# Deferring the operand forms of four plainly computed column pairs, and regrouping the second half of an MLP

## The chip, the core and the metric

The kernel runs on one core of a Trainium2 chip, as one launch. The metric is device time in microseconds. Engines are named as in the profile: PE is the matrix engine (PEld its weight loads), DVE the vector engine, ACT the scalar engine, POOL the general one, SP the engine on whose queue this kernel issues its DMAs.

## The reference

One step of a two-layer streaming encoder on 1024 prompt tokens and 32 sample tokens (1056 in all, width 1024, float32): layer 0 is a matrix-memory mixer with an MLP, layer 1 a banded attention with an MLP. The change lies in the MLP of layer 1 alone:

```python
x = layer_norm(ALPHA * x + (1 + g1) * y, p['ln_g'][l, 0], p['ln_b'][l, 0])
u = x * (1 + sc2) + sh2
f = jnp.square(jax.nn.relu(u @ p['w_up'][l])) @ p['w_down'][l]      # 1024 -> 4096 -> 1024
x = layer_norm(ALPHA * x + (1 + g2) * f, p['ln_g'][l, 1], p['ln_b'][l, 1])
```

## The kernel before, in words

**Arithmetic.** Every float32 operand is split into a high and a low part (`split`, L87: an ACT copy that rounds, then a DVE subtraction), and a product is three matmuls: high by high, high by low, low by high (`proj`, L110 to L120).

**The MLP of layer 1** (`mlp7`, from L1117) does most of its products with a seven-product scheme for 2 x 2 blocks in place of eight products. The 1056 tokens are four quarters of QN = 264; two quarters make a token pair `tp` (1: the later half, 0: the earlier one). The 4096 hidden columns are 16 column pairs `pb` of 256. A unit (pb, tp) in `Seven` (L1280) has seven products of 12 matmuls each (4 blocks of the contraction by 3). Its weights are seven combinations of the four blocks of a weight tile, made by `forms` (L1240): two loads on SP into the `raw` ring (3 buffers), four sums on DVE, seven splits, into the `wc` ring (6 buffers). Its moving operands are B11, B21, B22 and the combinations T1 to T4 of the activations u, which `tforms` (L1197) makes on DVE and ACT; the last of its steps writes T4 over the block B12 of u.

**Order of "up".** When the norm ahead of the MLP has finished the later half of the tokens, the column pairs 10 to 15 (`L.first`) are computed for that half "plainly", with eight products per block (`up_tile`, L1176; loops at L1313 and L1327); meanwhile the norm of the earlier half is still at work. The steps of `tforms` are spread between these blocks. Then the units follow in the order of `L.seq` (L1866): for the pairs 0 to 9 both token pairs, for 10 to 15 only the earlier half, the "lone" units. Neighbouring units are interleaved on PE by the sort at L1407. `prep` and `advance` (L1389, L1394) issue the weight loads two column pairs ahead and the forms one ahead. Only PE's order is written out by hand; on the other engines a scheduler of the framework lays the operations out, and each engine then works through its own queue in order.

**From "up" to "down".** When a unit or a plain pair is complete, `h_forms` (L1155) squares it on ACT, makes the three sums of the second half's operands on DVE, and splits all seven of them: four into the tile HL, three into HM (one buffer each), which SP stores to DRAM (`hd`). Pairs 14 and 15 (`pb >= NW`) only need a plain split into HL, stored to `hpl`.

**"Down"** takes the pairs 0 to 13 in groups (`GRP`, L1092: first pair and count): 3, 4, 3 and 4 pairs. For each group four units `m` (L1360) compute 256 output columns each, again with seven products, for both token pairs. The 14 operands of a group (7 for each token pair) are loaded into rooms, slots of freed buffers (`Rooms`, L1098; `fill`, L1353): 4 slots of the tile `ext` and 16 of the half of u that is finished are there before "up" ends, the rest after it. The results are added by DVE to the residual ACC (`L.add`, L986), which `L.reload` (L1419 and L1882) brings back from DRAM in four loads right after "up". At the end the pairs 14 and 15 are done plainly (from L1450), with the final norm behind them.

Of the kernel before, what the change touches and what calls it, by code (L numbers as in the profile page):

```python
# [8 lines left out]
F32 = mybir.dt.float32  # L9
# [6 lines left out]
P = 128  # L16
D = 1024
KC = D // P
# [57 lines left out]
def trunk_kernel(ctx: ExitStack, tc: tile.TileContext, a, o):  # L76
# [1012 lines left out]
    QN = T // 4  # L1089
    NPB, KG = 16, 4  # L1090
    NW = 14
    GRP = [(0, 3), (3, 4), (7, 3), (10, 4)]  # L1092
    B11, B22, B21, T1, T2, T4, T3, B12 = range(8)

    PRODS = [(0, B11, 0, 0, 0), (1, B21, 1, 0, 0), (2, T2, 0, 0, 1), (3, T1, 2, 1, 1), (4, T3, 0, 1, 1),
# [28 lines left out]
    def mlp7(L):  # L1124
# [9 lines left out]
        hpl = dr.tile([4, P, 2, T], F32, name=f"hpl{l}")  # L1134
        e_cm = tc.tile_pool(name=f"e{l}", bufs=1, reuse_waits="tile")
        ep = e_cm.__enter__()
        hh_cm = tc.tile_pool(name=f"hh{l}", bufs=1, reuse_waits="tile")
        hhp = hh_cm.__enter__()
        wups, hts = L.wups, {}
# [12 lines left out]
        def h_tile(pb, tp):  # L1152
            return hhp.tile([P, 6, QN], F32, tag="H", name=f"H{l}_{pb}_{tp}", bufs=3)

        def h_forms(pb, tp, H):  # L1155
# [9 lines left out]
            g = [i for i, (p0, kg) in enumerate(GRP) if p0 <= pb][-1]  # L1165
            dst = hd[g][tp][:, :, pb - GRP[g][0]].rearrange("f p l t -> p f (l t)")
            nc.vector.tensor_sub(H[:, 4:6], H[:, 0:3:2], bass.AP(H.tensor, H[:, 1].offset, [H.ap[0], [-QN, 2], [1, QN]]))
# [3 lines left out]
            nc.vector.tensor_sub(H[:, 3], H[:, 3], H[:, 1])  # L1171
            hm = hhp.tile([P, 3, 2, QN], F32R, tag="HM", name=f"HM{l}_{pb}_{tp}", bufs=1)
            split(hm[:, :, 0], hm[:, :, 1], H[:, 1:6:2])
            nc.sync.dma_start(dst[:, 4:7], hm.bitcast(F32).rearrange("p f l t -> p f (l t)"))

        def up_tile(pb, f, q):  # L1176

            tp = q // 2
            ps = up_mm(pb, f, q)
            if (pb, tp) not in hts:  # L1180
                hts[pb, tp] = [h_tile(pb, tp), 0]
            H = hts[pb, tp][0]
            nc.scalar.activation(H[:, ((1, 0), (3, 2))[f][q % 2]], ps, AF.Relu)
            hts[pb, tp][1] += 1
            if hts[pb, tp][1] == 4:
                h_forms(pb, tp, hts.pop((pb, tp))[0])
            flow.tick(QN / 96)

        def up_unit(pb, tp):
# [120 lines left out]

        tp0, tp1 = L.pairs

        TF = {}  # L1313
        for i in range(2):
            L.ready(i)
# [11 lines left out]
        for j, pb in enumerate(rest):  # L1327
            for f in range(2):
                for q in L.quarters[:2]:
                    up_tile(pb, f, q)  # L1330
                if (j, f) == (0, 1):
                    L.ready(2)
                    tiles = L.scratch()
                    TF.update({(tp, i): tiles[2 * n + i] for n, tp in enumerate(L.pairs) for i in range(2)})
                    exts[tp1] = ring.tile([P, 2, KG, QN], F32R, tag="wc", name=f"exu_{l}", bufs=6)
                    tfs = [tf, tforms(tp1, exts[tp1])]
                for n in ((), (0,), (0, 1), (0, 1), (1, 1), (1, 0, 1))[2 * j + f]:
                    next(tfs[n], None)
            del wups[pb]
            if j + 2 < len(rest):  # L1340
                up_w(rest[j + 2])
        def dn_forms(i):
            g, m, _ = units[i]
            p0, kg = GRP[g]
            return forms(lambda s_: w_dn[p0 * 256:(p0 + kg) * 256, m * 256:(m + 1) * 256].rearrange(
                "(k s p) c -> s p k c", s=2, p=P)[s_], kg, f"d{l}_{i}")

        fx, nfx = {}, {}
        order_f = [f for _, f, _, _, _ in PRODS]
        units = [(g, m, [(tp0,), (tp1,)] if g + m == 0 else [(tp0, tp1)]) for g in range(len(GRP)) for m in range(4)]  # L1350
        want = [(tp, f) for tp in L.pairs for f in order_f]

        def fill(g, into):  # L1353
# [27 lines left out]
                        step(i)  # L1381


        seq = L.seq
        jobs = [(n, tp) for n, (pb, tps) in enumerate(seq) for tp in tps]
        makers = [lambda pb=pb: up_forms(pb) for pb, _ in seq] + [lambda i=i: dn_forms(i) for i in range(len(units))]
        preps, got = {}, {}

        def prep(n):  # L1389
            if n < len(makers):  # L1390
                preps[n] = makers[n]()
                next(preps[n])

        def advance(n, i):  # L1394

            if n + 1 in preps and i in (0, 1, 3, 5):
                got[n + 1] = next(preps[n + 1])
            if i == 3:
                prep(n + 2)
        prep(0)  # L1400
        for _ in range(4):
            got[0] = next(preps[0])
        prep(1)
        lone = max(j for j, (_, tp) in enumerate(jobs) if tp == tp0) + 1
        sevens = {}
        with tc.manual_schedule(engines={mybir.EngineType.PE}):
            for _, j, i in sorted((7 * j + 2 * i, j, i) for j in range(len(jobs)) for i in range(7)):  # L1407
                n, tp = jobs[j]
# [451 lines left out]
    class L1:  # L1860
# [91 lines left out]
```

## Time and profile before

| | us |
|---|---|
| median of 3 timed runs (lowest to highest) | 2493.23 (2492.56 to 2494.87) |
| the profiled execution's own time | 2486.63 |
| its span, first to last instruction | 2484.8 |

The mean granted clock of PE in it was 0.984. Busy times by stage, of the profiled execution:

| stage, us from the start | length | PE | DVE | ACT | DMA share | GB/s |
|---|---|---|---|---|---|---|
| plain pairs, 1750.00 to 1787.56 | 37.56 | 37.56 | 37.46 | 32.01 | 0.61 | 214 |
| products of "up", 1827.80 to 2076.00 | 248.20 | 248.20 | 200.99 | 165.90 | 0.70 | 241 |
| its last units, 2076.00 to 2104.00 | 28.00 | 19.90 | 20.44 | 16.67 | 0.77 | 272 |
| start of "down", 2104.00 to 2143.30 | 39.30 | 21.28 | 18.69 | 8.15 | 1.03 | 390 |
| the rest of "down", 2143.30 to 2412.00 | 268.70 | 267.27 | 191.50 | 56.24 | 0.58 | 210 |
| pairs 14, 15 and the final norm, 2412.00 to 2484.80 | 72.80 | 58.69 | 52.80 | 15.09 | 0.32 | 118 |

How to read it: an engine whose busy time equals the length never waited. Matmuls are pipelined, so the duration of one in the trace is longer than the distance to the next; the distances between starts tell the rate. The DMA share is the mean busy share of the core's 16 DMA engines. In rows of the trace, a bracket at the end gives the idle time ahead of the row and what ended it.

### The profile page before, as it was taken

To read this page: it belongs to the slowest core of one execution; us is meant where nothing else is said; L and a number is where in the kernel's file an instruction comes from. 1 tells how busy PE (TensorE), PEld (TensorE's weight loads), DVE (VectorE), ACT (ScalarE), POOL (GpSimd) and SP (SyncE) were. 2 spreads that over 40 slices of the span, in tenths; PEclk is the share of its full clock that TensorE was granted. 3 is DMA by queue.
4 is the path that set the end of the run, shared out by engine and by line. 5 is a ranking of instruction groups with operands and counts; after the bars stand their busy time and mean duration, and the time that the engine had idled before them with its cause. 6 is when DMAs were issued, how large, how long until landed. Compare 5 with 4: busy or idle time off the path is not lost.

```text
span 2484.8 us, 42567 instructions
## 1 busy us (share of the span) xinstructions
PE 2386.1 (96%) x16532; PEld 2293.4 (92%) x16532; DVE 1888.6 (76%) x4228; ACT 1081.7 (44%) x2232; POOL 167.3 (7%) x315
## 2 busy tenths in 40 slices
PE   7999999999999999999999999999979998799997
PEld 4999999999999999999999877799979998799997
DVE  4899999778678778676597667738988888676758
ACT  4644456382211211211366567745756666121212
POOL 0211100000000000000001144400000000000003
PEclk9999999999999999999999999999989999899999
DMA  8433223313224224224123310052546678767632
GB/s 290 128 109 98 82 91 120 116 35 119 77 94 136 78 93 137 77 89 137 51 94 93 90 25 1 18 147 71 199 162 228 234 244 321 279 238 274 254 127 72
DMA packets 246766, 330.95 MB, mean 133 GB/s; under 512 B 12440, under 2 KB 197164, under 8 KB 245028
## 3 DMA queue, kind: packets, MB, share of 16 engines
q1 hardware_dynamic: 246564, 328.23, 39.8%
q8 instruction: 130, 2.13, 0.4%
q14 instruction: 72, 0.59, 0.1%
HBM read 251.31 MB, written 79.24 MB: 133 GB/s over the span
## 4 chain that ended last, share of the span: by engine, by line
PE 77%; DVE 10%; DMA 4%; ACT 2%; issue 1%; POOL 0%; SPq 0%; DVEq 0%; ACTq 0%; POOLq 0%
PE up L1297 10%; PE dn L1375 10%; PE up L118 5%; PE up L120 5%; PE up L119 5%; PE dn L119 5%; PE dn L118 5%; PE dn L120 5%; PE pv L1719 3%; PE s L1662 2%; PE pt L1697 2%; DMA fx<-hd 2%; PE op_a L118 1%; PE op_a L119 1%; PE op_a L120 1%
## 5 line engine op out<-in xcount | busy, mean ns | idle before, releaser
L1375 PE MATMUL dn<-fx,wf_d 128*128 128x264 f32 x2016 | 256.1, 286 | 19.4 <-DMA fx<-hd 16.4
L1375 PEld LDWEIGHTS dn<-fx,wf_d 128*128 128x128 f32 x2016 | 250.5, 190 | 22.0 <-DMA fx<-hd 15.0
L119 PE MATMUL dn<-h,w_dn 128*128 128x384 f32 (+1 forms) x768 | 249.5, 325 | 0.0
L118 PE MATMUL up<-U,w_up 128*128 128x384 f32 (+1 forms) x768 | 249.2, 325 | 0.0
L119 PE MATMUL up<-U,w_up 128*128 128x384 f32 (+1 forms) x768 | 247.9, 323 | 0.0
L118 PE MATMUL dn<-h,w_dn 128*128 128x384 f32 (+1 forms) x768 | 247.8, 323 | 0.0
L120 PE MATMUL up<-U,w_up 128*128 128x384 f32 (+1 forms) x768 | 247.6, 322 | 0.0
L120 PE MATMUL dn<-h,w_dn 128*128 128x384 f32 (+1 forms) x768 | 247.3, 322 | 0.0
L986 DVE SCALAR_TENSOR_TENSOR ACC<-dn,ada,ACC 128x264 f32<-128x264 f32 (+4 forms) x328 | 131.7, 426 | 94.9 <-PE dn L1375 81.8
L238 DVE SCALAR_TENSOR_TENSOR aacc<-rada,cs,aacc 128x256 f32<-128x256 f32 x448 | 190.2, 477 | 0.0
L1297 PE MATMUL up<-u,wf_u 128*128 128x264 f32 x1248 | 169.5, 289 | 20.5 <-ACT wf_u L89 16.5
L1297 PEld LDWEIGHTS up<-u,wf_u 128*128 128x128 f32 x1248 | 160.3, 192 | 22.1 <-ACT wf_u L89 17.2
L986 DVE SCALAR_TENSOR_TENSOR acc<-dn,ada,acc 128x384 f32<-128x384 f32 (+2 forms) x256 | 119.4, 486 | 48.3 <-PE dn L120 47.2
L1025 ACT ACTIVATE r<-up 128x384 f32<-128x384 f32 (+1 forms) x96 | 44.2, 462 | 246.1 <-PE up L120 237.6
L119 PEld LDWEIGHTS dn<-h,w_dn 128*128 128x128 f32 x768 | 144.5, 188 | 0.2 <-DVE h L1028 0.2
L120 PEld LDWEIGHTS dn<-h,w_dn 128*128 128x128 f32 x768 | 144.5, 188 | 0.0
L120 PEld LDWEIGHTS up<-U,w_up 128*128 128x128 f32 x768 | 144.3, 188 | 0.0
L118 PEld LDWEIGHTS up<-U,w_up 128*128 128x128 f32 x768 | 144.2, 188 | 0.1
L119 PEld LDWEIGHTS up<-U,w_up 128*128 128x128 f32 x768 | 144.2, 188 | 0.0
L118 PEld LDWEIGHTS dn<-h,w_dn 128*128 128x128 f32 x768 | 143.9, 187 | 0.2
L1027 DVE TENSOR_TENSOR r<-r 128x384 f32<-128x384 f32 (+1 forms) x96 | 50.0, 522 | 102.7 <-ACT h L1026 102.2
L89 ACT CAST w_up<-raw_up 128x1024 fp32r<-128x1024 f32 x44 | 46.0, 1047 | 134.6 <-DMA raw_up<-in_w_up_dram 105.8
(386 smaller groups left out, 6416.5 us busy)
## 6 DMA issues: line engine op xcount, KB each, us to landing
rada<-in_w_ada_dram SPq DMA_DIRECT2D x64, 512.0 KB
hd<-HL SPq DMA_DIRECT2D x28, 1056.0 KB
raw_up<-in_w_up_dram SPq DMA_DIRECT2D x44, 512.0 KB
hd<-HM SPq DMA_DIRECT2D x28, 792.0 KB
fx<-hd SPq DMA_DIRECT2D x35, 528.0 KB
raw_dn<-in_w_down_dram SPq DMA_DIRECT2D x36, 512.0 KB
ada_room<-in_w_ada_dram SPq DMA_DIRECT2D x32, 512.0 KB
rdn_u<-in_w_up_dram SPq DMA_DIRECT2D x32, 512.0 KB
```

The source lines that it names most:

```text
L89: nc.scalar.copy(dst_h, src)
L118: nc.tensor.matmul(ps, wh, mov(0, k), start=(k == 0), stop=False)
L119: nc.tensor.matmul(ps, wh, mov(1, k), start=False, stop=False)
L120: nc.tensor.matmul(ps, wl, mov(0, k), start=False, stop=(k == nk - 1))
L238: nc.vector.scalar_tensor_tensor(acc[:, cnd], raw[:, k], sc, acc[:, cnd], op0=ALU.mult, op1=ALU.add)
L986: nc.vector.scalar_tensor_tensor(xs, ps[:, off + o:off + o + mm_], gate[:, fc, cnd:cnd + 1], xs, op0=ALU.mult, op1=ALU.add)
L1027: nc.vector.tensor_mul(r, r, r)
L1297: nc.tensor.matmul(p, self.ws[w][:, wl, k], moving(f, tp, xl, k), start=first and k + n_ == 0, stop=k == 3 and n_ == 2, skip_group_check=n ...
L1375: nc.tensor.matmul(p, ws[w][:, wl, k], t[:, s0, xl], start=first and k + n_ == 0, stop=k == kg - 1 and n_ == 2, skip_group_check=not first)
L1662: nc.tensor.matmul(s[:, b, :w], qst, kk[i][:, g, k0 + j0:k0 + j0 + w], start=(i == 0), stop=(i == 1))
L1697: nc.tensor.transpose(pt[:kp, j - j0, pr * P:(pr + 1) * P], ps_[pr][:, j * P:j * P + kp], ident)
L1719: nc.tensor.matmul(pv[64 * e:64 * e + 64, :nq], V[:kp, vt0 + j, g * 64:(g + 1) * 64], pts[e][:kp, j, :nq], start=(j == 0), stop=(j == nt - 1))
```

## The change

- **Forms formed later.** For the plain pairs 10 to 13, `up_tile` no longer calls `h_forms`; SP stores the raw result (four blocks of 264, after the ReLU) to DRAM (`hraw`). A new generator `late` loads it back into a buffer of the `raw` ring, squares it, makes the sums and splits the seven operands one by one, each in a small tile of its own with its own store. One such job is spread over the first five products of a later half's unit; the first four column pairs carry one each.
- **Lone units spread.** The order becomes 0, 1, 10, 2, 3, 11, 4, 5, 12, 6, 7, 8, 9, 13, 14, 15, with the later half first for pair 0 too.
- **T forms.** The forms of the first weights (`prep(0)`) start during the last plain pair. The rest of the other half's `tforms` is issued after them, ahead of the first unit.
- **Groups of "down".** 2, 3, 3, 3 and 3 pairs. The second group's loads may start one unit earlier, with the second unit.
- **Residual.** One quarter is loaded right after "up", one more before each of the first three units.

`units`, `dn_forms`, `seq`, `jobs`, `makers`, `prep` and `advance` move up in the text without change.

```diff
-    GRP = [(0, 3), (3, 4), (7, 3), (10, 4)]
+    GRP = [(0, 2), (2, 3), (5, 3), (8, 3), (11, 3)]
...
+        hraw = {pb: dr.tile([P, 4, QN], F32, name=f"hraw{l}_{pb}") for pb in L.first if pb < NW}
...
+        def late(pb, tp):
+
+            H = raw_tile([P, 4, QN], f"hl_{l}_{pb}")
+            nc.sync.dma_start(H, hraw[pb])
+            yield
+            dst = h_place(pb, tp)
+
+            def put(f, src):
+                t = tmp_t([P, 2, QN], f"hf_{l}_{pb}_{f}", F32R)
+                split(t[:, 0], t[:, 1], src)
+                nc.sync.dma_start(dst[:, f], t.bitcast(F32).rearrange("p l t -> p (l t)"))
+            nc.scalar.activation(H, H, AF.Square)
+            put(B11, H[:, 1])
+            put(B22, H[:, 2])
+            yield
+            put(B21, H[:, 3])
+            nc.vector.tensor_sub(H[:, 1], H[:, 0], H[:, 1])
+            nc.vector.tensor_sub(H[:, 0], H[:, 2], H[:, 0])
+            put(T1, H[:, 1])
+            yield
+            nc.vector.tensor_sub(H[:, 2], H[:, 2], H[:, 1])
+            nc.vector.tensor_sub(H[:, 3], H[:, 3], H[:, 2])
+            put(T3, H[:, 0])
+            yield
+            put(T2, H[:, 2])
+            put(T4, H[:, 3])
+            yield
...
-                h_forms(pb, tp, hts.pop((pb, tp))[0])
+                H = hts.pop((pb, tp))[0]
+                if pb in hraw:
+                    nc.sync.dma_start(hraw[pb], H[:, 0:4])
+                else:
+                    h_forms(pb, tp, H)
...
-                for n in ((), (0,), (0, 1), (0, 1), (1, 1), (1, 0, 1))[2 * j + f]:
-                    next(tfs[n], None)
+                if (j, f) == (1, 1):
+                    prep(0)
+                for n in ((), (0,), (1, 1), (0,), (0, 2), (2, 2))[2 * j + f]:
+                    if n < 2:
+                        next(tfs[n])
+                    else:
+                        got[0] = next(preps[0])
...
-        prep(0)
-        for _ in range(4):
-            got[0] = next(preps[0])
+        next(tf, None)
         prep(1)
+        got[0] = next(preps[0])
+        for _ in tfs[1]:
+            pass
...
+        sevens, lates = {}, list(hraw)
...
                 if tp == seq[n][1][-1]:
                     advance(n, i)
+                elif lates:
+                    if i == 0:
+                        job = late(lates[0], tp0)
+                    if i < 5:
+                        next(job)
+                    if i == 4:
+                        del lates[0]
...
-        L.reload()
+        L.reload(0)
...
+                if i < 3:
+                    L.reload(i + 1)
...
-                if m == 2 and more:
+                if m == (2 if g else 1) and more:
                     fill(g + 1, nfx)
...
-        seq = [(pb, (0,) if pb > 9 else (1, 0) if pb else (0, 1)) for pb in (0, 1, 2, 14, 3, 4, 5, 15, 6, 7, 8, 10, 9, 11,
-                                                                             12, 13)]
+        seq = [(pb, (0,) if pb > 9 else (1, 0)) for pb in (0, 1, 10, 2, 3, 11, 4, 5, 12, 6, 7, 8, 9, 13, 14, 15)]
...
-        def reload():
-            x = acc["all"] = accp.tile([P, KC, T], F32, tag="acc", name="ACC2")
-            for k in range(0, KC, 2):
-                nc.sync.dma_start(x[:, k:k + 2], xsp[2][:, k:k + 2])
+        def reload(m):
+            if m == 0:
+                acc["all"] = accp.tile([P, KC, T], F32, tag="acc", name="ACC2")
+            nc.sync.dma_start(acc["all"][:, 2 * m:2 * m + 2], xsp[2][:, 2 * m:2 * m + 2])
```

`h_place` (not shown) is the address of a pair's operands in `hd`, cut out of `h_forms`.

More of the change, by code (lines that the diff above doesn't have):

```diff
@@ L1153, in h_tile, with h_place @@
             return hhp.tile([P, 6, QN], F32, tag="H", name=f"H{l}_{pb}_{tp}", bufs=3)
+        def h_place(pb, tp):
+            g = [i for i, (p0, kg) in enumerate(GRP) if p0 <= pb][-1]
+            return hd[g][tp][:, :, pb - GRP[g][0]].rearrange("f p l t -> p f (l t)")
+        def late(pb, tp):
[23 more added lines that the diff above has]
+            yield
         def h_forms(pb, tp, H):
@@ L1164, in h_forms @@
                 return
-            g = [i for i, (p0, kg) in enumerate(GRP) if p0 <= pb][-1]
-            dst = hd[g][tp][:, :, pb - GRP[g][0]].rearrange("f p l t -> p f (l t)")
+            dst = h_place(pb, tp)
             nc.vector.tensor_sub(H[:, 4:6], H[:, 0:3:2], bass.AP(H.tensor, H[:, 1].offset, [H.ap[0], [-QN, 2], [1, QN]]))
@@ L1311, in mlp7, with dn_forms, prep, advance @@
         tp0, tp1 = L.pairs
+        units = [(g, m, [(tp0,), (tp1,)] if g + m == 0 else [(tp0, tp1)]) for g in range(len(GRP)) for m in range(4)]
+        def dn_forms(i):
+            g, m, _ = units[i]
+            p0, kg = GRP[g]
+            return forms(lambda s_: w_dn[p0 * 256:(p0 + kg) * 256, m * 256:(m + 1) * 256].rearrange(
+                "(k s p) c -> s p k c", s=2, p=P)[s_], kg, f"d{l}_{i}")
+        seq = L.seq
+        jobs = [(n, tp) for n, (pb, tps) in enumerate(seq) for tp in tps]
+        makers = [lambda pb=pb: up_forms(pb) for pb, _ in seq] + [lambda i=i: dn_forms(i) for i in range(len(units))]
+        preps, got = {}, {}
+        def prep(n):
+            if n < len(makers):
+                preps[n] = makers[n]()
+                next(preps[n])
+        def advance(n, i):
+            if n + 1 in preps and i in (0, 1, 3, 5):
+                got[n + 1] = next(preps[n + 1])
+            if i == 3:
+                prep(n + 2)
         TF = {}
@@ L1341, in mlp7 @@
                 up_w(rest[j + 2])
[L1342 to L1346, printed above, removed]
         fx, nfx = {}, {}
         order_f = [f for _, f, _, _, _ in PRODS]
-        units = [(g, m, [(tp0,), (tp1,)] if g + m == 0 else [(tp0, tp1)]) for g in range(len(GRP)) for m in range(4)]
         want = [(tp, f) for tp in L.pairs for f in order_f]
@@ L1381, in unit @@
                         step(i)
[L1384 to L1399, printed above, removed]
-        prep(0)
-        for _ in range(4):
-            got[0] = next(preps[0])
+        next(tf, None)
         prep(1)
+        got[0] = next(preps[0])
+        for _ in tfs[1]:
+            pass
         lone = max(j for j, (_, tp) in enumerate(jobs) if tp == tp0) + 1
-        sevens = {}
+        sevens, lates = {}, list(hraw)
         with tc.manual_schedule(engines={mybir.EngineType.PE}):
```

## Prediction, on record before the changed kernel ran

> **What bounds the kernel now.** I read the page first (span, costliest groups), then the busy times by stage, then PE's waits in order of time.
>
> ```profile
> span 2484.8 us, 42567 instructions
> L1375 PE MATMUL dn<-fx,wf_d 128*128 128x264 f32 x2016 | 256.1, 286 | 19.4 <-DMA fx<-hd 16.4
> L1297 PE MATMUL up<-u,wf_u 128*128 128x264 f32 x1248 | 169.5, 289 | 20.5 <-ACT wf_u L89 16.5
> ```
>
> Both large groups of the last stage are matmuls, and each has some 20 us of idle in front of it: "up" waited for weight splits, "down" for operand loads. The stage table shows where (columns: window, its length, busy us and count of PE, PEld, DVE, ACT, POOL, then granted clock, DMA share, GB/s).
>
> ```profile
> 1787.56:1832.13 44.57, 25.59 (x137) 23.93 (x138) 40.78 (x44) 20.84 (x32) 0.00 (x0) 0.66 0.53 176
> 1900.00:2000.00 100.00, 100.00 (x824) 100.00 (x823) 79.90 (x134) 67.49 (x116) 0.00 (x0) 1.00 0.69 237
> 2076.00:2092.00 16.00, 7.90 (x46) 7.38 (x45) 9.83 (x16) 7.95 (x13) 0.00 (x0) 0.68 0.88 315
> 2104.00:2141.00 37.00, 18.98 (x122) 17.10 (x122) 16.68 (x37) 6.92 (x11) 0.00 (x0) 0.77 1.03 390
> ```
>
> Undisturbed, 824 matmuls take 100 us: 0.1214 each, 1.46 us for a product of 12, 10.2 for a unit of 84. By that the 137 matmuls of the first window are worth 16.6 us, and it loses about 28; the third (46, so 5.6) loses 10.4; the fourth (122, so 14.8) loses 22.2. In the first DVE is 91% busy and is the bound; in the fourth it is the DMA (share 1.03). These 60 us are what the change can reach.
>
> ```profile
> 1790.95 0.59 PE L120 MATMUL up<-u,w_up 128*128 128x264 f32 x1 [3.39 <-DVE w_up L90]
> 1796.83 0.42 PE L118 MATMUL up<-u,w_up 128*128 128x264 f32 x1
> 1797.05 0.34 PE L119 MATMUL up<-u,w_up 128*128 128x264 f32 x1
> 1812.44 0.81 PE L1297 MATMUL up<-u,wf_u 128*128 128x264 f32 x2 [7.73 <-ACT wf_u L89]
> 1817.02 2.57 PE L1297 MATMUL up<-u,wf_u 128*128 128x264 f32 x10 [3.77 <-DVE wf_u L90]
> 1820.52 3.30 PE L1297 MATMUL up<-u,wf_u 128*128 128x264 f32 x12 [0.94 <-ACT wf_u L89]
> 1825.81 0.81 PE L1297 MATMUL up<-TF,wf_u 128*128 128x264 f32 x2 [1.99 <-ACT wf_u L89]
> 1827.78 4.50 PE L1297 MATMUL up<-TF,wf_u 128*128 128x264 f32 x22 [1.17 <-DVE wf_u L90]
> 1832.13 1.61 PE L1297 MATMUL up<-u,wf_u 128*128 128x264 f32 x12
> 2085.54 0.81 PE L1297 MATMUL up<-u,wf_u 128*128 128x264 f32 x2 [7.81 <-ACT wf_u L89]
> 2102.96 1.63 PE L1375 MATMUL dn<-fx_e,wf_d 128*128 128x264 f32 x12
> 2125.96 1.03 PE L1375 MATMUL dn<-fx,wf_d 128*128 128x264 f32 x3 [12.85 <-DMA fx<-hd]
> ```
>
> **A. The front, -27 us.** DVE's effective prices are distances between neighbouring starts:
>
> ```profile
> 1754.96 0.70 DVE L1167 TENSOR_TENSOR H<-H 128x528 f32<-128x528 f32 x1
> 1755.58 1.25 DVE L1207 TENSOR_TENSOR t<-u 128x1056 f32<-128x1056 f32 x1
> ...
> 1790.81 0.42 DVE L1171 TENSOR_TENSOR H<-H 128x264 f32<-128x264 f32 x1
> 1791.15 1.22 DVE L90 TENSOR_TENSOR w_up<-raw_up,w_up 128x1024 fp32r<-128x1024 f32 x1
> 1792.29 0.97 DVE L90 TENSOR_TENSOR HM<-H,HM 128x792 fp32r<-128x792 f32 x1
> 1793.18 2.42 DVE L1207 TENSOR_TENSOR t<-u 128x1056 f32<-128x1056 f32 x2
> ...
> 1819.27 1.26 DVE L90 TENSOR_TENSOR TF<-t,TF 128x1056 fp32r<-128x1056 f32 x1 [1.14 <-ACT TF L89]
> 1820.50 0.69 DVE L90 TENSOR_TENSOR wf_u<-rdn_u,wf_u 128x512 fp32r<-128x512 f32 x1
> ...
> 1824.05 0.68 DVE L1262 TENSOR_TENSOR s_u<-s_u,rdn_u 128x512 f32<-128x512 f32 x1
> 1824.65 0.68 DVE L1263 TENSOR_TENSOR s_u<-rdn_u 128x512 f32<-128x512 f32 x1
> 1825.27 1.26 DVE L90 TENSOR_TENSOR u<-t,u 128x1056 fp32r<-128x1056 f32 x1
> 1826.44 0.68 DVE L1264 TENSOR_TENSOR s_u<-rdn_u,s_u 128x512 f32<-128x512 f32 x1
> ```
>
> That is 0.62 us for 528 columns, 1.17 for 1056, 0.34 for 264, 0.89 for 792, 0.60 for 512. The forms of one plain pair (528, 1056, twice 264, 792) cost 3.36, the four of them 13.4. The second split of the first weights ended at 1821.2. From ahead of it go the 13.4; by the built order of the changed program twelve operations of 1056 (seven of the other pair's T forms, four of the first pair's, one HL) come behind it, 14.0; and the wait of 1.14 goes. So it ends near 1792.7, and PE becomes the later one. Its stall of 3.39 goes too (the split that ended it stood behind three of the four pairs' forms). The 96 matmuls of the last plain block, 11.7 us, then start at 1787.6, and the products at 1799.2. Before, they stood as if begun at 1832.13 - 48 x 0.1214 = 1826.3. Difference 27. ACT sheds four squares and eight copies there.
>
> **B. The deferred forms, +19 us.** Late after 1799 is DVE. Seven more of 512 and three of 1056 bring it to 1800.5; there the T form written over u must wait for the plain matmuls. Nine of 1056, four of 512 and four of 264 later (14.3), with 1.5 for ACT's copies, stands the T form of the second unit's third product: 1816.3, against PE's 1799.2 + 8 x 1.46 = 1810.9. First stall 5.4.
>
> Each deferred pair adds 4 subtractions and 7 splits of 264 (3.7 us of DVE), a square and 7 copies on ACT, a load and 7 stores. The square holds ACT's queue until the load has landed; the PSUM copies of the next products wait behind it, and PE for those. On SP the weight loads of the next-but-one pair stand behind the seven stores, each of which waits for DVE. And the load shares the three raw buffers, so the first waits for the last T form, at about 1821.
>
> ```profile
> 1806.60 3.12 DMA hpl<-HL
> 1815.50 4.32 DMA rdn_u<-in_w_up_dram
> ```
>
> A weight load of 512 KB lands after 4.3 us, a store of 264 KB after 3.1. So the load of 528 KB is there near 1826; square, copies and the eleven forms, between other work, end near 1834; the next pair's third weight (two sums and a split, 1.8) is ready at 1835.5. PE, undelayed, wants it at 1799.2 + 15 x 1.46 = 1821.1: 14.4 late. From there DVE is full: four pairs of 6.6 (weights) + 8.8 (sums and forms) + 3.7, and two lone units of 11, are 98 us in the 102 of ten units, so nothing is won back and little more is lost. I add 2.7 for a clock ramp and 2 for waits on loads: +19. Bounds: +10 if copies and loads are hidden, +43 by the DMA (rival 3).
>
> After the idle of 3.39 the next matmuls start 0.22 apart until 1797.05, and 0.12 after: some 28 matmuls, 2.7 us lost. The Trainium skill, TensorE: Matmul & The Clock Gate (Part 1: The HAM clock gate), says that about 3.4 us of idle halves the clock and about 3.4 us of work restores it. By that rule the ramp would cost 1.7 us, and B be 18; here the slow stretch lasts 6.1 us, so the trace's number stands.
>
> **C. The stall near the end of "up", +1.** The chain of waits, then ACT's timeline:
>
> ```profile
> 2072.47 8.24 DMA hd<-HL
> 2080.78 1.08 ACT HL L89
> ```
> ```profile
> 2084.87 1.28 ACT L89 CAST wf_u<-rdn_u 128x512 fp32r<-128x512 f32 x2
> ```
>
> ACT's copy into the single HL buffer waits until the previous HL has landed, behind the fill of the first down group; the last unit's weight splits stand behind it, so PE waits 7.81. The new order has the same row of operations, units 13 and 15 for 11 and 13, and the fill just ahead is larger: six loads of 528 KB for 2640 KB, 540 KB more at that window's 315 GB/s, 1.7 us. I take +1; -10 if the slack that DVE has by then frees it, +4 above.
>
> **D. The start of "down", -7.5.**
>
> ```profile
> 2117.61 12.55 SPq L1117 DMA_DIRECT2D fx<-hd  x11
> ```
> ```profile
> hd<-HL SPq DMA_DIRECT2D x28, 1056.0 KB
> hd<-HM SPq DMA_DIRECT2D x28, 792.0 KB
> fx<-hd SPq DMA_DIRECT2D x35, 528.0 KB
> ```
>
> Now six of 14 operands are in; the missing loads are issued from 2117.6, behind the last HL and HM stores and all four residual quarters. Changed: ten of 14 are in (two pairs each), 7.3 us of work for PE; the last units, 14 and 15, store only HL. With "up" ending at 2103 as before: square, wait for the previous HL, copy and subtraction end near 2111; then four stores, a quarter, and the four missing loads, 1056 + 1056 + 4 x 528 KB, 4.3 MB. At 390 GB/s that is 11 us, so 2122 to 2124. Unit 0 ends near 2125.5 instead of 2113.2: 12.3 lost, with 2.4 for the ramp 14.7, against 22.2. Three of the four quarters still stand ahead of those loads; the spreading takes one out of the way (2.8 us, in the sum). Bounds: -14 (loads at once) and +2 (the next group's 13 loads delay the fourth unit's weights, which stand behind them).
>
> **E. Five groups instead of four, +2.** The matmuls are as many. A unit of two pairs is 10.2 us of PE, with eleven form operations of 256 columns and 14 sums in 18 pieces on DVE, at most 29 x 0.34 = 9.9 us: covered, barely. Bounds 0 and +8.
>
> **The sum:** -27 + 19 + 1 - 7.5 + 2 = -12.5 us, on the profiled span of 2484.8. That execution took 2486.63; the median of the three timed runs is 2493.23, 6.6 above it, and I subtract from the median: **2480.7 us**.
>
> **Rivals.**
> 1. *DVE and ACT keep up.* B is 12, the stall of C goes (-8), D is -12, E 0: -35, 2458 us. For it: DVE is 80% busy in the steady window. Against: the first deferred pairs meet the moved T forms. Chance 0.15.
> 2. *No change.* B is 31, because the square of each deferred pair holds ACT's queue 3 us longer than I count (4 x 3): what the front gains is given back. 2493 us. Chance 0.20. That the change doesn't do what it says belongs here: three quarters stay ahead of the loads, and the HL stall recurs.
> 3. *Slower: the DMA fills up.* A deferred pair moves 528 + 7 x 264 = 2376 KB besides the pair's 1024 + 2 x 1848; four of these and two lone units (2872 each) make 34.9 MB in 102 us, 342 GB/s. The steady window moved 237 GB/s at a share of 0.69, which is 343 at a share of 1: no room. Below 261 GB/s the stretch takes 133.5 us, B passes 31.5, and the sign turns; at 240 it takes 145, B is 43, the sum +11.5: 2505 us. For it: weights and stores share one ordered queue. Against: 390 GB/s in the fourth window. Chance 0.20.
>
> **How the numbers follow.** The forecast has 0.45 and its own range, 2468 to 2488. The range of 8 in 10 takes in rival 2, half of 3 and half of 1: 2456 to 2503. About 0.2%, 5 us, is what a measurement of this kernel tells from no change. Faster: forecast and rival 1, 0.60; within: 0.20; slower: 0.20.
>
> **What would show it.** A: no PE idle from 1787 to 1799, and the products follow within 3 us. B: idle of PE between 1809 and 1840, released by TF or wf_u, then DVE over 90% busy until about 1920. C: one idle of 8 to 10 us before the last unit, behind an HL store. D: one idle of about 9 us, 7 us after "down" begins, released by fx. It is wrong if the products run without idle from 1799, if the DMA share stands at 1 through the first 100 us of products, or if PE idles inside the first down group.

## The result, and the profile after

| | median us (lowest to highest) | runs |
|---|---|---|
| before | 2492.6 (2490.9 to 2495.9) | 10 |
| changed | 2507.4 (2498.7 to 2513.5) | 10 |

The changed kernel takes 1.0054 times as long (95% interval 1.0039 to 1.0068): **14.8 us slower**, where 12.5 us faster was forecast. It lies outside the range, 4 us above its upper end.

From the page of the changed kernel, the large groups of matmuls in this MLP (at the end of a row: the idle time ahead of the group, and what ended most of it):

```profile
span 2505.2 us, 42905 instructions
L1433 PE MATMUL dn<-fx,wf_d 128*128 128x264 f32 x2016 | 257.3, 287 | 17.5 <-DMA fx<-hd 8.4
L1333 PE MATMUL up<-u,wf_u 128*128 128x264 f32 x1248 | 170.5, 291 | 12.2 <-ACT wf_u L89 9.2
L1333 PE MATMUL up<-TF,wf_u 128*128 128x264 f32 x624 | 93.2, 301 | 20.3 <-ACT wf_u L89 8.9
```

The idle ahead of the "up" products has moved: 20.5 us stood ahead of the group that reads u, now it is 12.2, but the group that reads the T forms went from 3.2 to 20.3. Ahead of "down" stand 17.5 us, before 19.4; waits for operands (`fx<-hd`) were 16.4 of it before and are 8.4 now, so other waits have come in.

To compare stages, the traces need a common zero, since their beginnings differ. The last statistics matmul of the norm ahead of the MLP serves (first and last start are the last two times of the row); in the kernel before, the same matmul starts at 1762.8:

```profile
L864 PE MATMUL var_n<-qr_n,ones_d x18: 292/336/689, 478.5 to 1766.7; 128*128 128x384 f32 x12, 128*128 128x288 f32 x6
```

Now PE in order of time (start, length, and in brackets the idle ahead of the row):

```profile
1802.07 3.11 PE L1333 MATMUL up<-u,wf_u 128*128 128x264 f32 x24
1807.76 4.44 PE L1333 MATMUL up<-TF,wf_u 128*128 128x264 f32 x22 [2.58 <-ACT H L1336]
...
1822.47 0.59 PE L1333 MATMUL up<-TF,wf_u 128*128 128x264 f32 x1 [4.21 <-ACT TF L89]
...
1843.20 0.81 PE L1333 MATMUL up<-TF,wf_u 128*128 128x264 f32 x2 [7.10 <-ACT wf_u L89]
...
1900.03 0.51 PE L1333 MATMUL up<-TF,wf_u 128*128 128x264 f32 x2 [1.32 <-ACT wf_u L89]
1902.14 1.61 PE L1333 MATMUL up<-TF,wf_u 128*128 128x264 f32 x10 [1.59 <-DVE wf_u L90]
1904.58 3.01 PE L1333 MATMUL up<-u,wf_u 128*128 128x264 f32 x12 [0.83 <-DVE H L1339]
1907.38 2.84 PE L1333 MATMUL up<-TF,wf_u 128*128 128x264 f32 x12
...
1931.36 3.01 PE L1333 MATMUL up<-u,wf_u 128*128 128x264 f32 x12 [1.90 <-DVE H L1339]
...
2099.82 0.81 PE L1333 MATMUL up<-u,wf_u 128*128 128x264 f32 x2 [9.16 <-ACT wf_u L89]
...
2117.11 1.62 PE L1433 MATMUL dn<-fx_e,wf_d 128*128 128x264 f32 x12
...
2135.07 5.02 PE L1433 MATMUL dn<-fx,wf_d 128*128 128x264 f32 x24 [8.37 <-DMA fx<-hd]
...
2161.72 4.52 PE L1433 MATMUL dn<-fx,wf_d 128*128 128x264 f32 x19 [4.58 <-DVE ACC L986]
...
2433.14 0.58 PE L118 MATMUL dn<-hs,w_dn 128*128 128x288 f32 x1 [3.17 <-DMA hs<-hpl]
```

Three things are to be seen. The products begin at 1802.07 without a stall, 35.4 us after the zero; before, the first stood at 49.6 with stalls behind it, and counted back from where they run freely it is as if they had begun at 63.5. Then come stalls that were not there: one at the third product (1807.76, ended by an ACT copy), one at a T form (1822), one of 7.10 before the second pair's weights (1843), and small clusters at 1900 to 1905 and 1926 to 1931. And behind each of these five places the clock is low: two products start 2.80 and 2.65 us apart at 1904.58 and 1907.38, where 1.46 is the rule. The stage table (granted clock third from the end) says the same:

```profile
1802.07:1850.00 47.93, 32.34 (x211) 31.11 (x210) 36.65 (x54) 23.80 (x41) 0.00 (x0) 0.79 0.50 168
...
1898.00:1940.00 42.00, 35.20 (x234) 33.82 (x234) 32.90 (x62) 27.33 (x49) 0.00 (x0) 0.84 0.75 262
```

The ledger of the two profiled executions, in us:

| stage | before | after | difference | forecast |
|---|---|---|---|---|
| start of the trace to the zero | 1762.8 | 1766.7 | +3.9 | - |
| zero to the products, "as if begun" (A) | 63.5 | 35.4 | -28.1 | -27 |
| from there to the end of "up" (B, C) | 276.7 | 315.0 | +38.3 | +20 |
| "down" to pairs 14, 15 (D, E) | 311.5 | 316.0 | +4.5 | -5.5 |
| the rest | 70.4 | 72.1 | +1.7 | 0 |

It sums to 20.3, and the spans differ by 20.4; the medians differ by 14.8, because the profiled execution of before lay 6 us under its median and that of after on it. The first row need not be the change's: in experiments 3 and 10, whose first half is that of before, the zero lies at 1767.2 and 1769.0. The 2184 matmuls of "up" (26 units of 84) are worth 265.1 us at 0.1214, so 49.9 are lost there in the changed kernel: 32.5 as idle, the rest to the low clock.

### The profile page after: what moved, and what is told of

Its sections match the earlier page's. It is cut to its first block, busy times and chain, and to the rows that moved or that the text cites. A ratio compares the mean times of both kernels' runs of the same rounds, so it can differ in the third digit from the quotient of the medians.

```text
span 2505.2 us, 42905 instructions
## 1 busy us (share of the span) xinstructions
PE 2400.9 (96%) x16532; PEld 2307.3 (92%) x16532; DVE 1925.2 (77%) x4368; ACT 1090.4 (44%) x2280; POOL 166.6 (7%) x315
## 4 chain that ended last, share of the span: by engine, by line
PE 74%; DVE 11%; DMA 5%; ACT 3%; issue 2%; POOL 1%; SPq 0%; ACTq 0%; DVEq 0%; POOLq 0%
PE dn L1433 11%; PE up L1333 7%; PE up L118 5%; PE up L119 5%; PE up L120 5%; PE dn L119 5%; PE dn L118 5%; PE dn L120 5%; PE pv L1771 3%; PE s L1714 2%; PE pt L1749 2%; PE o L118 1%; PE o L119 1%; PE o L120 1%; PE op_b L118 1%
## 5 line engine op out<-in xcount | busy, mean ns | idle before, releaser
L1433 PE MATMUL dn<-fx,wf_d 128*128 128x264 f32 x2016 | 257.3, 287 | 17.5 <-DMA fx<-hd 8.4
L986 DVE SCALAR_TENSOR_TENSOR ACC<-dn,ada,ACC 128x264 f32<-128x264 f32 (+5 forms) x400 | 160.5, 428 | 72.4 <-PE dn L1433 54.2
L1333 PE MATMUL up<-u,wf_u 128*128 128x264 f32 x1248 | 170.5, 291 | 12.2 <-ACT wf_u L89 9.2
L1333 PE MATMUL up<-TF,wf_u 128*128 128x264 f32 x624 | 93.2, 301 | 20.3 <-ACT wf_u L89 8.9
```

The costliest lines, as they stand in the source:

```text
L986: nc.vector.scalar_tensor_tensor(xs, ps[:, off + o:off + o + mm_], gate[:, fc, cnd:cnd + 1], xs, op0=ALU.mult, op1=ALU.add)
L1333: nc.tensor.matmul(p, self.ws[w][:, wl, k], moving(f, tp, xl, k), start=first and k + n_ == 0, stop=k == 3 and n_ == 2, skip_group_check=n ...
L1433: nc.tensor.matmul(p, ws[w][:, wl, k], t[:, s0, xl], start=first and k + n_ == 0, stop=k == kg - 1 and n_ == 2, skip_group_check=not first)
```

## The experiments

Medians and ratios are against the kernel before on the same chip, which took 2492.9 to 2493.9 us in these comparisons.

**1. No deferral.**

```diff
-        hraw = {pb: dr.tile(...) for pb in L.first if pb < NW}
+        hraw = {}
```

> The changed kernel, but with the forms of all plain pairs made at once, as before; order of the units, place of the T forms, groups and residual stay changed. Theory 1 (the deferred forms cause the idle of the first 140 us of products: DVE and ACT have no room for them beside the weights there): the 36 us lost between 1802 and 1940 go, the products begin some 14 us later because DVE has the 13.4 us of sums and splits again ahead of the first weights; 2507 - 36 + 14 = about 2485 us. Theory 2 (the moved T forms and the spread lone units make that idle, with or without the deferred forms): at most 8 us come back and 14 are lost, 2505 to 2520 us.

Measured: 2496.8 us, 1.0014 (1.0005 to 1.0022). Of the changed kernel's 2507.4 us 10.6 come back, and nothing but the deferral was undone: as it is done here, it makes the kernel slower than forming at once. But it falls short of the 22 that theory 1 expected: the T forms and the last unit still stall (5.5 and 11.6 us in its trace), and the second half is the changed one.

**2. and 3. The order alone, the second half alone, on the kernel before.**

```diff
-        seq = [... (0, 1, 2, 14, 3, 4, 5, 15, 6, 7, 8, 10, 9, 11, 12, 13)]
+        seq = [... (0, 1, 10, 2, 3, 11, 4, 5, 12, 6, 7, 8, 9, 13, 14, 15)]
```

> The kernel before with the changed order of the units alone (0, 1, 10, 2, 3, 11, 4, 5, 12, 6, 7, 8, 9, 13, 14, 15, later half first throughout). Theory 1 (the spread order costs nothing by itself): 2490 to 2496 us, no idle of PE over 2 us between 1832 and 2076. Theory 2 (a lone unit, 11 us of DVE in 10.2 of PE, so early leaves no reserve and makes idle): 2500 us or more, with idle around 1865 and 1900. The stall before the last unit (7.8 us) stays by both.

Measured: 2492.7 us, 1.0001 (0.9992 to 1.0010). The order of the units alone costs nothing, and from 1835 to 2080 PE has no idle in its trace.

```diff
-    GRP = [(0, 3), (3, 4), (7, 3), (10, 4)]
+    GRP = [(0, 2), (2, 3), (5, 3), (8, 3), (11, 3)]
...
-        L.reload()
+        L.reload(0)
...
+                if i < 3:
+                    L.reload(i + 1)
...
-                if m == 2 and more:
+                if m == (2 if g else 1) and more:
...
 # and L.reload by quarters, as in the change
```

> The kernel before with only the new groups of the second half (2, 3, 3, 3, 3), the second group's loads one unit earlier, and the residual in quarters. The second half took 316.0 us in the changed kernel and 309.8 before. Theory 1 (the small first group pulls the next group's loads ahead of the weights, and units of two pairs leave DVE no reserve: the 6 us are the change's own): about 2499 us. Theory 2 (the 6 us come from the state in which the first half ends, its last stores and loads): the first wait falls from 12.9 to about 9 us and nothing else is added, about 2487 us.

Measured: 2500.8 us, 1.0036 (1.0022 to 1.0050). The second half was forecast to gain 5.5 and costs 7.9 by itself.

**4. The deferred jobs on the column pairs 6 to 9 instead of 0 to 3.**

```diff
-                elif lates:
+                elif lates and n > 8:
```

> The changed kernel with the four deferred jobs on the column pairs 6, 7, 8 and 9 instead of 0, 1, 2 and 3: behind the last T forms, and with no lone unit beside them. Theory 1 (the place is wrong: in the first ten units DVE is already filled by T forms, weights and lone units): of the 36 us lost in the first 140 us of products some 5 to 8 stay (the T form over u), the later pairs need 6.6 + 8.8 + 3.7 = 19.1 of DVE in 20.4 us and lose little; about 2480 us. Theory 2 (the extra operations cost wherever they are, by DVE's and ACT's queues or by the DMA): the idle moves to 1985 to 2070, about 2505 us.

Measured: 2509.8 us, 1.0066 (1.0054 to 1.0078). Theory 1 of this run falls: in the first half of the MLP the later place is no better than the first ten units. The small stalls came along with the jobs, and the one before the last unit is 12.67 (PE of this kernel):

```profile
2045.77 1.74 PE L1333 MATMUL up<-u,wf_u 128*128 128x264 f32 x12 [1.90 <-DVE H L1339]
2066.81 1.48 PE L1333 MATMUL up<-TF,wf_u 128*128 128x264 f32 x10 [1.54 <-DVE wf_u L90]
2069.65 3.01 PE L1333 MATMUL up<-u,wf_u 128*128 128x264 f32 x12 [1.36 <-DVE H L1339]
2087.97 3.29 PE L1333 MATMUL up<-u,wf_u 128*128 128x264 f32 x12 [12.67 <-ACT wf_u L89]
```

**5. to 7. What in a job costs: its engine work, its transfers, nothing.**

```diff
 # engine work alone: other data, no load, no stores in the job
-            nc.sync.dma_start(H, hraw[pb])
-            nc.scalar.activation(H, H, AF.Square)
+            nc.scalar.activation(H, L.u4(0, tp, 0, 0).bitcast(F32), AF.Square)
...
-                nc.sync.dma_start(dst[:, f], t.bitcast(F32).rearrange("p l t -> p (l t)"))
...
 # four transfers store raw data where the operands belong, behind the plain pair
```

> The changed kernel with only the engine work of the deferred jobs left in them: square, sums and splits of four raw blocks at the same places, in the same ring buffer, but on other data (a block of u) and without the load and the seven stores. In their stead four transfers store raw data where the operands belong, right behind the plain pair; so this kernel leaves out the forms of four pairs. Theory 1 (the idle comes from the time of DVE and ACT and from the order of their queues): it stays, 2502 to 2508 us. Theory 2 (it comes from SP's queue and the transfers: weight loads behind seven stores, the load that holds ACT): most of the 36 us goes, 2480 to 2488 us.

```diff
 # transfers alone: no square, no sums, no splits
-                t = tmp_t([P, 2, QN], f"hf_{l}_{pb}_{f}", F32R)
-                split(t[:, 0], t[:, 1], src)
-                nc.sync.dma_start(dst[:, f], t.bitcast(F32).rearrange("p l t -> p (l t)"))
+                nc.sync.dma_start(dst[:, f], H[:, f % 3:f % 3 + 2].rearrange("p l t -> p (l t)"))
```

> The reverse: the deferred jobs keep the load and the seven stores, at the same places, but the stores take the raw blocks as they are; square, sums and splits are left out, so the forms of four pairs are not computed. Theory 1 (DVE and ACT): the idle that the four jobs make goes, and only the T form's first stall and the one before the last unit stay; 2480 to 2488 us. Theory 2 (SP and the transfers): 2502 to 2508 us.

```diff
 # no job at all: four transfers store raw data where the operands belong, behind the plain pair
-                elif lates:
...
```

> The changed kernel without any deferred job: right behind each plain pair four transfers store its raw data where the operands belong, and nothing more is done; the forms of four pairs are left out. With the jobs whole it is 2507.4, with their engine work alone 2495.8, with their transfers alone 2490.6 us. If the two halves cost independently of each other, this gives 2495.8 + 2490.6 - 2507.4 = 2479 us (2476 to 2482). If they are coupled (a store that waits for DVE holds the weight loads behind it on SP, so the whole costs more than its halves), it is higher, 2484 to 2490 us.

Measured: engine work alone 2495.8 us (1.0007, 0.9998 to 1.0015), transfers alone 2490.6 (0.9989, 0.9980 to 0.9997), nothing 2488.0 (0.9976, 0.9967 to 0.9985). So, against the kernel without jobs, the four jobs cost 19.4 us; their engine work alone 7.8, their transfers alone 2.6, and 9.0 only appear when both are there. Neither theory of the first two runs had it: each half alone is cheap. (In experiments 5 and 7 the four raw stores stand in for the seven of a job, so their transfers are not none.)

**8. The job's transfers on GpSimd's queue.**

```diff
-            nc.sync.dma_start(H, hraw[pb])
+            nc.gpsimd.dma_start(H, hraw[pb])
...
-                nc.sync.dma_start(dst[:, f], ...)
+                nc.gpsimd.dma_start(dst[:, f], ...)
```

> The changed kernel with the load and the seven stores of each deferred job on GpSimd's queue, which has nothing else to do there, in place of SP's; all else the same. Theory 1 (order in SP's queue: the weight loads stand behind stores that wait for DVE): 2495 to 2501 us. Theory 2 (the transfers themselves, or DVE and ACT): 2505 to 2510 us.

Measured: 2519.0 us, 1.0107 (1.0094 to 1.0120), above both theories. Waits of DVE and ACT from 1800 to 1945 in its trace (total, times, longest):

```profile
DVE s_u L1300 <- DMA hd<-hf: 8.6, 3, 3.1
```
```profile
ACT hl L1171 <- DMA hl<-hraw: 5.5, 3, 3.4
```

A new wait: sums of the weights (`s_u`) now wait until operand tiles `hf` have been stored, because both take their buffers from one ring of five. And the square (L1171) waits longer for its load. So this run doesn't clear SP's queue, since it brings a wait of its own; but it points at the load.

**9. The job without its wait for the load.**

```diff
-            nc.sync.dma_start(H, hraw[pb])
+            nc.sync.dma_start(hcopy[pb], hraw[pb])
-            nc.scalar.activation(H, H, AF.Square)
+            nc.scalar.activation(H, L.u4(0, tp, 0, 0).bitcast(F32), AF.Square)
```

> The changed kernel with the deferred jobs' engine work and their seven stores at their places, but on other data (a block of u), so that the square waits for no load; the load becomes a copy of the same size from DRAM to DRAM, free to go early. The forms of four pairs are thereby wrong data. No job 2488.0, engine work alone 2495.8, transfers alone 2490.6, whole job 2507.4: 9 us more than the two halves explain. Theory 1 (those 9 us come from the data: the square stands in ACT's queue until the load is there, the sums on DVE come late, and DVE, some 95% busy, can't make it good): they go, 2496 to 2500 us. Theory 2 (they come from the stores: each waits for DVE and holds SP's queue, and their tiles share a ring with the weight sums): they stay, 2505 to 2509 us.

Measured: 2495.0 us, 1.0002 (0.9993 to 1.0010): 12.4 less than the whole job, and no more than its engine work alone. The seven stores are all there, on SP, each behind DVE, and cost nothing that can be seen. The stalls up to the second pair's weights stay; this is the last of them, 7.10 in the changed kernel:

```profile
1844.24 0.81 PE L1333 MATMUL up<-TF,wf_u 128*128 128x264 f32 x2 [6.33 <-ACT wf_u L89]
```

The gain lies behind it. In the same 90 us, the changed kernel and then this one (third and fourth busy times: DVE, ACT):

```profile
1850.00:1900.00 50.00, 48.06 (x393) 47.63 (x391) 44.81 (x85) 38.48 (x71) 0.00 (x0) 1.00 0.80 286
1900.00:1940.00 40.00, 34.50 (x228) 33.33 (x229) 30.90 (x58) 26.09 (x47) 0.00 (x0) 0.83 0.75 261
```
```profile
1850.00:1900.00 50.00, 49.36 (x405) 49.15 (x405) 46.38 (x89) 38.39 (x71) 0.00 (x0) 1.00 0.80 284
1900.00:1940.00 40.00, 38.73 (x319) 38.52 (x318) 38.01 (x71) 30.91 (x57) 0.00 (x0) 1.00 0.88 306
```

With data at hand DVE is busy 84.4 of 90 us and PE waits 1.9; with the load in the chain DVE is busy 75.7 and PE waits 7.4, with a low clock behind it. What DVE waited for from 1850 to 1940, the same two kernels:

```profile
DVE wf_u L90 <- ACT wf_u L89: 5.8, 3, 3.8
DVE HL L90 <- ACT HL L89: 4.1, 4, 1.8
```
```profile
DVE HM L90 <- ACT HM L89: 2.5, 2, 1.6
DVE wf_u L90 <- ACT wf_u L89: 1.1, 2, 0.7
```

It waited for ACT longer, and the chain of waits of the changed kernel shows how:

```profile
1881.84 0.61 DVE wf_u L90
1882.47 5.79 DMA hl<-hraw
1888.29 1.10 ACT hl L1171
...
1893.20 1.10 ACT H L1190
1894.32 0.72 DVE H L1199
...
1897.69 0.69 DVE s_u L1297
```

The load can only start when DVE has read out the weights that held the ring buffer (1881.84); it lands 5.79 us later; then the square and the job's copies stand in ACT's queue ahead of the square of a whole unit (L1190), whose sums stand in DVE's queue ahead of the next pair's weights. One limit remains: with nothing to wait for, the copies in this experiment also stand earlier in SP's queue, so the place of the load and the wait for it aren't told apart. Nor does the chain say how much of the 12.4 us each of its steps is worth.

**10. to 12. The second half taken apart.**

```diff
 # on the kernel before
-    GRP = [(0, 3), (3, 4), (7, 3), (10, 4)]
+    GRP = [(0, 2), (2, 3), (5, 3), (8, 3), (11, 3)]
```

> The kernel before with the new groups 2, 3, 3, 3, 3 alone; residual in one go, next group's loads at the third unit as before. The same with all of the changed second half took 2500.8 against 2492.9 us. Theory 1 (five smaller groups cost by themselves: a first group that waits as long as before, DVE without reserve in units of two pairs, the last loads later): 2498 to 2502 us. Theory 2 (the quarters of the residual and the earlier loads in SP's queue cost): 2491 to 2495 us.

```diff
 # on the changed kernel
-                if m == (2 if g else 1) and more:
+                if m == 2 and more:
```

> The changed kernel, but the second group's loads come with the third unit of the first group, as before, in place of the second. Theory 1 (the wait of 4.6 us in the third unit comes from weights whose loads stand behind the next group's operands): that wait goes, with some 2 us of slow clock; 2499 to 2502 us, and the wait for the last groups is as it was. Theory 2 (DVE without reserve in units of two pairs): unchanged, 2505 to 2509 us, and the wait stays.

```diff
 # on the changed kernel
-    GRP = [(0, 2), (2, 3), (5, 3), (8, 3), (11, 3)]
+    GRP = [(0, 3), (3, 4), (7, 3), (10, 4)]
 # and L.reload, its calls and the condition of fill as before
```

> The changed kernel with the second half as before: groups of 3, 4, 3 and 4 pairs, second group's loads with the third unit, residual in one go. On the kernel before the changed second half cost 7.9 us (2492.9 to 2500.8). Theory 1 (it costs this also behind the changed first half): 2507.4 - 7.9 = 2499.5 us (2497 to 2502), and the first wait for operands is longer than the 8.4 us of the changed kernel. Theory 2 (behind the changed first half the smaller first group pays, as forecast, 5.5 us): 2511 to 2515 us.

Measured: the groups alone 2497.9 us (1.0016, 1.0007 to 1.0025), just under theory 1. The second group's loads at the third unit 2504.3 (1.0047, 1.0034 to 1.0060). In its trace the wait of 4.58 in the third unit is gone, as theory 1 said; what is left is one of 2.36 in the fourth unit, where the changed kernel has 1.35:

```profile
2170.66 4.53 PE L1433 MATMUL dn<-fx,wf_d 128*128 128x264 f32 x24 [2.36 <-DVE ACC L986]
```

The medians are 3.2 us apart, but the two intervals overlap, and the changed kernel's own runs spread over 15 us: the wait is explained, its price in time is not settled. The old second half behind the changed first half 2497.0 (1.0017, 1.0008 to 1.0026): the changed second half costs 10.4 us there. PE's waits in "down", first with the old second half, then with the changed one:

```profile
PE dn L1433 <- DMA fx<-hd: 13.4, 5, 10.9
PE dn L1433 <- DVE ACC L986: 1.7, 3, 0.7
```
```profile
PE dn L1433 <- DMA fx<-hd: 8.4, 1, 8.4
PE dn L1433 <- DVE ACC L986: 8.1, 5, 4.6
PE dn L118 <- DMA hs<-hpl: 3.2, 1, 3.2
PE dn L1433 <- ACT wf_d L89: 2.1, 2, 1.3
```

The wait for operands does get shorter, by 5.0. Waits for DVE, for the last loads and for weights take 13.4 where 2.0 were (with 0.3 before the last loads), and slow clock follows the longest (0.58 from 2161.72 to 2167). The profiled execution of experiment 12 was its fastest, 4.6 us under its median.

**13. and 14. The jobs in the second half.** If a job costs because DVE has no reserve, it belongs where it has one, and the old fourth group holds exactly the four deferred pairs.

```diff
 # the first half changed, without the jobs; old groups, residual and loads
+                def step(j):
+                    advance(nu + i, j)
+                    if g == 1 and j < 5:
+                        if j == 0:
+                            jobs[m] = late(lates[m], tp0)
+                        next(jobs[m])
```

> The changed front and order of units with the old groups (3, 4, 3, 4), residual and loads; the four deferred jobs are moved behind the whole first half, one into each unit of the second group of the second half, where DVE is 71% and ACT 21% busy; their operands are needed from the fourth group on. Theory 1 (a deferred job costs what DVE and ACT have no room for at its place): nothing of the 36 us stays but the stall on the T form over u, some 8 with its slow clock; the second half as before; 2507 - 36 + 8 - 6 = about 2473 us. Theory 2 (the jobs cost 10 us or more wherever they stand): 2490 us or more.

Measured: 2486.4 us, 0.9962 (0.9950 to 0.9975), 7 us faster than before, 13 short of theory 1. In its trace the first half ends 325.9 us after the zero (before 340.2, changed kernel 350.4). The first two stalls are there without any job:

```profile
1807.31 4.43 PE L1333 MATMUL up<-TF,wf_u 128*128 128x264 f32 x24 [2.86 <-ACT H L1336]
1822.50 0.59 PE L1333 MATMUL up<-TF,wf_u 128*128 128x264 f32 x1 [4.94 <-ACT TF L89]
```

But "down" takes 323.2 instead of 308.4 in the kernel of experiment 12: PE waits 19.5 us for operands, not 13.4, so at least 6 us of the gain are lost again to the wait for transfers; the rest of the 14.8 was not followed up.

```diff
 # in addition
-                if j == lone - 1 and i == 6:
+                if j == lone + 1 and i == 6:
```

> The version with the four jobs in the second half (2486.4 us), with the first fill of the second half's operands issued two units later. Theory 1 (the stall before the last unit, 9.3 us, is the store of HL that lands behind that fill): the stall falls below 3 us, the start of the second half loses a few of them again; 2478 to 2483 us. Theory 2 (the operands then come too late): what the stall gives back is lost in the first wait of the second half, 2485 to 2492 us.

Measured: **2480.2 us, 0.9951** (0.9939 to 0.9963), 13.3 us faster than before and 27 faster than the changed kernel. The stall before the last unit is gone; 4.2 us stand at the first unit of "down" instead, for its weights, and the waits for operands are no longer (total, times, longest; 19.5 in experiment 13):

```profile
PE dn L1433 <- DMA fx<-hd: 15.2, 8, 9.8
```

## Why the prediction was wrong, step by step

- **A, the front: right.** Forecast -27, traced -28.1. No idle between 1787 and 1799, DVE no longer the bound ahead of the first weights.
- **B, the deferred forms: the step that failed.** In the changed trace B is 36.5 where +19 was forecast: at the front 7.5 us of idle (2.58, 4.21 and 0.70), from the second pair to 1931 another 15.5, and five stretches of low clock, at the forecast's price of 2.7 each 13.5 (by the granted clock of 5 to 7 us behind each stall 13.9). The first stall was forecast rightly: the T form of the second unit's third product, 4.21 + 0.70 for 5.4. The 2.58 was not in the sum: it ends with ACT's copy of a product's result (L1336, at 1807.33), which stands in ACT's queue behind the square and the HL copy of a plain pair (1804.87 and 1806.36). Both stalls come with the moved front and not with the jobs, since experiment 13 has them too (2.86 and 4.94 + 0.70). The jobs are the rest: from the first product to the end of "up" it takes 315.0 us with them and 290.6 in experiment 13.

  Two terms were too small. The sum counts *one* clock ramp, "2.7 for a clock ramp", and there were five: 10.8 us missing. And the rest of the idle was taken as settled once the second pair's weights had come (PE had them at 1843.2, forecast 1835.5; 3.9 of the difference is the later zero), because DVE was to be full: "nothing is won back and little more is lost". It was not full. Of the time from 1802 to 1940 DVE was busy 112.4 of 138 us, where "over 90% busy until about 1920" was to show the mechanism; it waited. Without the wait for the load (experiment 9) the idle and the low clock from 1850 on all but go, and this is worth the 9 to 12 us of experiments 7 and 9. The forecast let the stall before the second pair's weights hang on the load too; but it is 6.33 where the square waits for no load (experiment 9).
- **Rival 2 came nearest in B**, with 31, and it named the place, the deferred pair's square in ACT's queue. Its reason is borne out only in part: it had ACT held 3 us longer per pair, and ACT waited 2.0 us for the loads in all. The chain of experiment 9 points to the order instead, in which what stands behind the square comes late. The clock ramps and the second half it left out, so that its total, 2493, is 14 us short.
- **Rival 3 had nearly the time, 2505, and the wrong mechanism**, so that was luck. Over the stretch the DMA was not full: a share of 0.68 from 1802 to 1940, 0.80 and 287 GB/s from 1850 to 1898 (only single windows of some us reach 1), and experiment 9 runs at 0.88 and 306 GB/s from 1900 to 1940 with hardly a wait of PE. The transfers alone cost 2.6.
- **C, the stall near the end of "up": right.** One idle of 9.16, behind an HL store, before the last unit, 1.4 more than the 7.81 of before; forecast +1. Experiment 14 shows that the first fill ahead of it makes the stall.
- **D, the start of "down": right in itself.** One idle of 8.37, released by fx (forecast about 9); it ends 18.0 us after "down" begins (forecast 19 to 21). The waits for operands fall from 16.4 to 8.4, by 8.0 (forecast 7.5, with the ramps).
- **E, five groups: the other step that failed.** Forecast +2, at most +8. With the shorter wait for operands taken off, it is 4.5 + 1.7 + 8.0 = 14 against the profiled execution of before, and 10.4 + 5.0 = 15 against experiment 12 (medians, and its trace's 13.4 of such waits). That PE idles inside the first group was one of the signs of being wrong. The sum reckoned DVE's work and not the order around it. The bound that D named, "the next group's 13 loads delay the fourth unit's weights", is what the trace of the changed kernel shows, and it was left out of the value. SP's queue, then the chain:

```profile
2127.97 16.58 SPq L1117 DMA_DIRECT2D fx<-hd  x16
...
2147.17 4.43 SPq L1281 DMA_DIRECT2D rdn_d<-in_w_down_dram  x2
```
```profile
2147.17 10.57 DMA rdn_d<-in_w_down_dram
2157.83 0.41 ACT wf_d L89
```

  The weights are issued behind sixteen operand loads and land after 10.57 us; their splits stand in DVE's queue ahead of the additions to ACC, which free PE's result banks; so PE waits 4.58 for "DVE ACC" in the third unit. With the loads later that wait is gone (experiment 11). The order alone does not fix its size: in experiment 3, where sixteen loads stand ahead of the weights as well, it is 1.06. The last loads (`hs`) came 3.17 late, nowhere in the sum. The rest of the second half's loss, small waits for DVE and for weights, was not settled one by one, and how much of the 14 to 15 us each part is worth stays open.

## What to carry to other kernels

Work that is moved off an engine's crowded stretch is only cheap where the engines have time for the work *and* for its wait: here a step that begins with a load delayed what was queued behind it, and an engine with 84 us of work in 90 could not make that good. The same jobs in the second half left the kernel faster than before. Count stalls, not only their length: by the granted clock the five of the first half cost 1.7 to 3.2 us on top of their idle. And when a refill is brought forward, look at what it now stands ahead of in the issuing queue.

## What the runs showed of the hardware

The clock falls after idle in pieces, too. In the changed kernel idles of 1.32, 1.59 and 0.83 us within six, none of them long, are followed by products 2.8 us apart, and the single 2.58 at 1807.76 by a granted clock of 0.66 (from 1807 to 1812). The Trainium skill, TensorE: Matmul & The Clock Gate (Part 1: The HAM clock gate), has the clock halve after an idle window of about 3.4 us; the first three sum to 3.74, but 2.58 is less. A sum alone doesn't decide either: in experiment 4 idles of 0.61, 0.65 and 1.90 left the clock at 1.00, and 1.54 and 1.36 were followed by 0.54, as 0.51, 0.64 and 1.90 were in the changed kernel (0.54 from 1931 to 1938; granted clock third from the end):

```profile
2045.00:2052.00 7.00, 6.23 (x51) 6.23 (x52) 4.77 (x9) 5.03 (x9) 0.00 (x0) 1.00 0.83 296
...
2069.00:2076.00 7.00, 5.65 (x24) 5.34 (x24) 2.94 (x6) 3.41 (x6) 0.00 (x0) 0.54 0.97 310
```

Why these cases differ is open.
